# Down projection of a two-layer decoder: residual loads in half slices, kept weight blocks loaded with their partners, casts behind the sums, squares moved into slice 0's steps, and its norm in buffers of its own

## The chip, the cores and the metric

One core of one Trainium2 chip. TensorE (PE in the rows) multiplies; PEld is its weight load; VectorE (DVE), ScalarE (ACT) and GpSimd (POOL) do the elementwise work; SyncE (SP) and GpSimd issue the DMAs here. The metric is device microseconds of one execution, the median over runs. All times below are microseconds (us).

## The reference, cut to what matters

The program is one step of a two-layer decoder in fp32. Layer 0 is an mLSTM mixer, layer 1 an attention with forget gates; each is followed by the same kind of feed-forward block, and between the layers a shared key/value projection is made from the normed result of layer 0:

```
h = h + mixer_l(rmsnorm(h))                       # l = 0: mLSTM, l = 1: attention
h = h + swiglu(rmsnorm(h), w_gate_up[l], w_down[l])
        # gu = xn @ w_gu ;  (silu(gu[:, :2816]) * gu[:, 2816:]) @ w_d
after layer 0:  k, v, lf from  rmsnorm(h, norm_kv) @ w_kvf
after layer 1:  y = rmsnorm(h, norm_final)
```

The model width is 1024, the hidden width 2816. There are 1104 tokens: 64 of the sample group, 16 meta tokens, 1024 of the prompt.

## The kernel before, in words

**Tiling.** Activations lie transposed, width on the 128 partitions: the residual H of a token slice is a tile of 128 x 8 x 368 (8 chunks of the width, 368 tokens). There are three slices, t = 0, 1, 2. The program's names for the tiles of H are vA in layer 0 and Ht in layer 1 (in the issue order vA_83, vA_84, vA_85 are the areas of slices 0, 1, 2). An fp32 product is made of three fast ones: each operand is split into a high part (a cast on ACT, L331) and a low part (a subtraction on DVE, L332), and hi*hi, hi*lo, lo*hi are accumulated in PSUM.

**Down stage.** `ffn` runs twice. Its last part is the product with w_down, a list of 61 steps; each step is 24 matmuls (4 output chunks x 2 contraction chunks x 3 products, L1949). Steps 0 to 38 compute slices 1 and 2 by a scheme of Strassen's kind: seven "rounds" named r2, r5, r3, r1, r6, r7, r4 of five steps each, with four plain steps between (5, 6, 17, 18). A round multiplies sums of hidden slices (made earlier and put into DRAM as hA) with sums of weight blocks. Steps 39 to 60 are slice 0, plain, in two halves of the width. A step whose entry has an `out` ends an accumulation: DVE adds the four PSUM banks into H (L1492). A step with `lead` takes fresh banks, and there are four banks, so the lead step after an out step waits for these adds.

**What each step issues, in this order:** the split of the weight block needed two steps later (`w_split`: cast on ACT, low part on DVE); the split of the hidden block needed two steps later (`h_split`) and the load of the block three after it (`h_load`, POOL's queue, tile hr, three buffers with the tag ny, so that a load waits for the low part of the block three before it); the sum of the next weight block where the round needs one (`w_sum`, DVE, L1493), ahead of the matmuls in a step without `out`, behind the adds in a step with it; the 24 matmuls; the adds; the load of a weight block three ahead (`w_load`, SP's queue). The rounds r5, r1, r7, r4 need sums. The blocks that several rounds share are kept in the tile wx; five of them (`kept[1, q]`) are loaded in steps 3 to 7's calls of `w_load`, behind each call's own block.

**Residuals.** H was put into DRAM (hD) to make room, and comes back by POOL's queue at L1969: slice 1 is issued at step 1, slice 2 at step 3, slice 0 at step 8 of the program. PE, DVE and ACT run in the order in which the program is written; the order on the queues of POOL and SP is the scheduler's, which may put a DMA elsewhere.

**Squares and norm.** As the chunks of H are finished, a list `pend` collects their squares (`each`, which calls `add_sq`: ACT squares, L400 and L403, POOL adds into ns, L405, and DVE does the last add). One is taken from it at each step without an out before step 39 and two from there on. When a slice is complete its generator (`norm_x` in layer 0, `final` in layer 1) is appended, and `advance` takes one piece of it per step in steps 39 to 49, two from step 50. `norm_x` is a matmul with ones (L413), a square root, three reciprocals (L419), and for each chunk a multiplication, a cast and a subtraction (L425, L426, L428; for slice 0 four pieces of two chunks, L433, L439, L441, over the same three ny buffers). Behind the last step of layer 0 come the first products of the key/value projection (L269 to L271), whose weights are scaled by L325 and L326 and whose results are copied by L2054 and sent out by POOL.

Of the kernel before, what the change touches and what calls it, by code (L numbers as in the profile page):

```python
# [7 lines left out]
F32 = mybir.dt.float32  # L8
# [244 lines left out]
class Net:  # L253
# [153 lines left out]
    def norm_x(self, H, t, g, sp, pp, inplace=False, psum=False):  # L407
# [15 lines left out]
        for k in range(KT if psum else 0):  # L423
            y = pp.tile([P, 512], F32, name=self.uid("npy"), tag="n")[:, :n]
            nc.vector.tensor_tensor(out=y, in0=H[t][:, k], in1=r, op=ALU.mult)  # L425
            nc.scalar.copy(xh[:, k], y)  # L426
            yield
            nc.vector.tensor_tensor(out=xl[:, k], in0=y, in1=xh[:, k].bitcast(F32), op=ALU.subtract)  # L428
        for z in range(0 if psum else 4):
            ks = slice(2 * z, 2 * z + 2)  # L430
            y = H[t][:, ks] if inplace else self.ny(self.uid("ny"))[:, : 2 * n].rearrange("p (k n) -> p k n", k=2)
# [8 lines left out]
            yield  # L440
            nc.vector.tensor_tensor(out=xl[:, ks, :], in0=y, in1=xh[:, ks, :].bitcast(F32), op=ALU.subtract)  # L441
# [37 lines left out]
    def mlp(self, H, w, l, heads=None, cb=None, early=None):  # L479
# [8 lines left out]
        with self.pool(self.uid("nsp")) as sp, self.pool(self.uid("npp"), bufs=2, space=PSUM) as pn:  # L488
# [3 lines left out]
            def small(c, down=False):  # L492
                p = c.enter_context(self.pool(self.uid("small")))
                if down:
                    nq = p.tile([P, 1 if l else 2, SL], F32, name=self.uid("nq"))
                    self.nq = lambda x: self.nr if l and x else nq[:, x]
                    self.ny = lambda nm: p.tile([P, 2 * SL if l else max(2 * SL, 3 * 256)], F32, name=nm, tag="ny", bufs=3)
# [107 lines left out]
            with cw if not cb else ExitStack():  # L605
# [8 lines left out]
                if cb:  # L614
                    def after(t):
                        nc.gpsimd.dma_start(self.hD[:, :, TS[t][0] : TS[t][1]], H[t])
                        return self.norm_x(H, t, None, sp, pn, psum=t > 0)
# [847 lines left out]
def ffn(self, H, flat, l, weights, order, mix, small, each, after, end, early=None):  # L1465
# [10 lines left out]
    with self.pool(f"ffn{l}") as fp, self.pool(f"ffnp{l}", space=PSUM) as pp:  # L1476
# [220 lines left out]
        def w_load(i):  # L1697
            if i < len(ws):
# [18 lines left out]
                if 3 <= i < 3 + NR:  # L1717
                    keep_w(1, i - 3, 0, 0)
# [13 lines left out]

        def w_split(i):
            if i < len(ws):
                p = (i + max(0, min(3, (i - 19) // 5))) % 4
                wpart[i] = tuple(view(self.slots[y]) for y in (2 + p, LOW[p]))
                self.split(wraw.pop(i), *wpart[i])
# [143 lines left out]
        with fixed(E.DVE, E.Activation):  # L1881
# [24 lines left out]
            wr = dp.tile([P, KT * P], F32, name=f"wr{l}")  # L1906
            fin = None if after else self.final_setup(dp)
# [18 lines left out]
            for i, (wi, hi, lead, out) in enumerate(seq):  # L1926
# [9 lines left out]
                if todo and not out:  # L1936
                    w_sum(todo + 1)
# [25 lines left out]
                if todo and out:  # L1963
                    w_sum(todo + 1)
                if todo:
                    w_load(todo + 3)
                if i in (1, 3, 8):
                    y = {1: 1, 3: 2, 8: 0}[i]
                    nc.gpsimd.dma_start(H[y], self.hD[:, :, TS[y][0] : TS[y][1]])  # L1969
                for _ in range(0 if i < NX else 1 if i < NX + NC else 2):  # L1970
                    advance()
                if not out:
                    for _ in range(1 if i < NX else 2):
# [996 lines left out]
```

## Time and profile before

| | |
|---|---|
| three runs | 2869.14, 2859.06, 2856.49 us |
| median | 2859.06 us |
| profiled execution: time, span | 2863.41 us, 2861.7 us (1.7 us outside of the span) |
| granted clock of TensorE, mean | 0.989 |
| PE busy | 2755.9 us, 96% |
| DVE, ACT, POOL busy | 1869.1, 1317.8, 1105.6 us |
| DMA | 415.06 MB, mean 145 GB/s |
| down stage of layer 0, profile time | about 1003 to 1255 us, then the tail up to about 1300 |
| down stage of layer 1, profile time | about 2574 to 2849 us |

Rows of a timeline read: start, duration, engine, line, operation, output tile <- input tiles, shape, count, and in brackets the idle time of that engine just before and the instruction whose end ended it. Rows of windows give, for a stretch, the busy time of each engine with the number of instructions, the granted clock of TensorE (1.00 is full), the share of the DMA engines and the GB/s.

### The profile page before, as it was taken

To read this page: it belongs to the slowest core of one execution; us is meant where nothing else is said; L and a number is where in the kernel's file an instruction comes from. 1 tells how busy PE (TensorE), PEld (TensorE's weight loads), DVE (VectorE), ACT (ScalarE), POOL (GpSimd) and SP (SyncE) were. 2 spreads that over 40 slices of the span, in tenths; PEclk is the share of its full clock that TensorE was granted. 3 is DMA by queue.
4 is the path that set the end of the run, shared out by engine and by line. 5 is a ranking of instruction groups with operands and counts; after the bars stand their busy time and mean duration, and the time that the engine had idled before them with its cause. 6 is when DMAs were issued, how large, how long until landed. Compare 5 with 4: busy or idle time off the path is not lost. (4 is left out here: it accounts for less than half of the span.)

```text
span 2861.7 us, 54039 instructions
## 1 busy us (share of the span) xinstructions
PE 2755.9 (96%) x20390; PEld 2621.2 (92%) x20390; DVE 1869.1 (65%) x3790; ACT 1317.8 (46%) x2652; POOL 1105.6 (39%) x1612
## 2 busy tenths in 40 slices
PE   7999999999999989999999999999999999999998
PEld 7998988999999989999999888777999999998998
DVE  6044566688888766762465543777478888876673
ACT  6222464444444433442344454777344454443342
POOL 3042333065656312217573201455307566531220
PEclk9999999999999999999999999999999999999999
DMA  6157664122332385644453676452412223238463
GB/s 208 30 139 174 164 177 153 53 88 92 97 100 86 115 314 157 223 143 142 137 170 115 236 286 226 138 170 88 157 50 91 94 92 106 84 125 314 140 227 100
DMA packets 321207, 415.06 MB, mean 145 GB/s; under 512 B 30183, under 2 KB 244691, under 8 KB 319923
## 3 DMA queue, kind: packets, MB, share of 16 engines
q1 hardware_dynamic: 282114, 281.63, 30.9%
q0 software_dynamic: 38080, 129.43, 14.3%
q8 instruction: 160, 2.62, 0.4%
q14 instruction: 101, 0.82, 0.1%
q10 hardware_dynamic: 752, 0.57, 0.1%
HBM read 303.46 MB, written 108.07 MB: 144 GB/s over the span
## 5 line engine op out<-in xcount | busy, mean ns | idle before, releaser
L1949 PE MATMUL dps<-x0h,slot 128*128 128x368 f32 x1440 | 366.7, 334 | 19.0 <-DVE vA L1492 9.7
L1949 PEld LDWEIGHTS dps<-x0h,slot 128*128 128x128 f32 x1440 | 258.9, 190 | 22.4 <-issue 21.0
L332 DVE TENSOR_TENSOR slot<-slot,slot 128x256 fp32r<-128x256 f32 (+2 forms) x233 | 211.2, 908 | 68.3 <-ACT slot L331 63.5
L331 ACT CAST slot<-slot 128x256 fp32r<-128x256 f32 (+2 forms) x233 | 175.0, 754 | 163.7 <-PE m L1516 66.8
L1949 PE MATMUL dps<-x0l,slot 128*128 128x368 f32 x720 | 239.1, 332 | 1.0 <-DVE x0l L332 1.0
L1516 PE MATMUL m<-x1h,slot 128*128 128x368 f32 x640 | 180.0, 335 | 3.3 <-DVE ns L1493 0.9
L1516 PE MATMUL m<-x0h,slot 128*128 128x368 f32 x640 | 178.5, 329 | 0.0
L1949 PEld LDWEIGHTS dps<-x0l,slot 128*128 128x128 f32 x720 | 136.7, 190 | 1.3 <-DVE x0l L332 1.2
L111 POOL TENSOR_TENSOR slot<-Ht 128x256 f32<-128x256 f32 x80 | 75.4, 954 | 151.4 <-DMA Ht<-in_w_gate_up 79.8
L111 POOL TENSOR_TENSOR slot<-vA 128x256 f32<-128x256 f32 x80 | 75.4, 953 | 148.8 <-DMA vA<-in_w_gate_up 76.7
L1516 PE MATMUL m<-x2h,slot 128*128 128x368 f32 x480 | 132.3, 330 | 0.0
L1516 PEld LDWEIGHTS m<-x1h,slot 128*128 128x128 f32 x640 | 116.0, 188 | 12.4 <-DVE ns L1493 7.4
L332 DVE TENSOR_TENSOR slot<-Ht,slot 128x256 fp32r<-128x256 f32 (+3 forms) x101 | 91.5, 907 | 52.3 <-ACT slot L331 52.3
L332 DVE TENSOR_TENSOR slot<-vA,slot 128x256 fp32r<-128x256 f32 (+3 forms) x101 | 92.1, 913 | 50.3 <-ACT slot L331 50.3
L1669 POOL DMA_DIRECT2D hr<-hA x62 | 33.7, 543 | 217.6 <-DVE x0l L332 177.8
L1516 PEld LDWEIGHTS m<-x0h,slot 128*128 128x128 f32 x640 | 116.0, 188 | 0.0
L405 POOL TENSOR_TENSOR ns<-ns,nq 128x368 f32<-128x368 f32 x50 | 63.1, 1262 | 129.7 <-ACT nq L403 125.0
L1516 PE MATMUL m<-x1l,slot 128*128 128x368 f32 x320 | 105.5, 330 | 0.0
L1516 PE MATMUL m<-x0l,slot 128*128 128x368 f32 x320 | 105.4, 329 | 0.0
L2764 ACT ACTIVATE s<-s,nb 128x272 f32<-128x272 f32 (+7 forms) x126 | 98.8, 786 | 0.0
L2799 ACT COPY th<-tp 128x768 f32<-128x768 f32 (+1 forms) x80 | 73.5, 920 | 49.2 <-PE tp L2791 27.9
L1516 PE MATMUL m<-T_2h,slot 128*128 128x368 f32 x320 | 93.8, 334 | 0.0
(858 smaller groups left out, 9619.6 us busy)
## 6 DMA issues: line engine op xcount, KB each, us to landing
slot<-in_w_down SPq DMA_DIRECT2D x64, 512.0 KB, 4.4
hr<-hA POOLq DMA_DIRECT2D x62, 368.0 KB, 4.1
wraw<-in_w_in_a SPq DMA_DIRECT2D x40, 512.0 KB, 4.4
vA<-in_w_gate_up SPq DMA_DIRECT2D x40, 512.0 KB, 3.9
Ht<-in_w_gate_up SPq DMA_DIRECT2D x40, 512.0 KB, 4.0
wr<-in_w_down SPq DMA_DIRECT2D x32, 512.0 KB, 3.8
kp<-in_cache_k SPq DMA_DIRECT2D x32, 512.0 KB, 6.8
vp<-in_cache_v SPq DMA_DIRECT2D x32, 512.0 KB, 7.6
```

The costliest lines, as they stand in the source:

```text
L111: self.net.nc.gpsimd.tensor_tensor(out=o, in0=a, in1=b, op=op)
L331: self.nc.scalar.copy(hi, src)
L332: self.nc.vector.tensor_tensor(out=lo, in0=src, in1=hi.bitcast(F32), op=ALU.subtract)
L405: (nc.vector if x >= late else nc.gpsimd).tensor_tensor(out=s, in0=s, in1=sq, op=ALU.add)
L1516: nc.tensor.matmul(u.b[b][:, :SL], w[p][:, k], x[q][:, k], start=new and k == i == 0, stop=k == 1 and i == 2, skip_group_check=True)
L1669: nc.gpsimd.dma_start(hraw[j], src)
L1949: nc.tensor.matmul(o, w[:, k, ms], a[:, k], start=lead and k == x == 0, stop=k == 1 and x == 2, skip_group_check=True)
L2764: nc.scalar.activation(ss[z, u], ss[z, u], AF.Exp, bias=nb[:, z : z + 1], accum_out=sm[:, u, z : z + 1])
L2799: nc.scalar.copy(th.rearrange("p x z (u h q) -> p h (x z u) q", h=2, q=64)[:, :, :n], pt[:, :, :n])
```

## The change

1. The residual of slice 1 comes back in two halves of four chunks (program steps 1 and 11), that of slice 2 too (steps 2 and 7), that of slice 0 whole at step 24.
2. The five kept blocks are loaded by the calls of `w_load` that load the blocks of round r5 they are summed with, instead of by the calls 3 to 7.
3. `w_sum` always stands behind the matmuls and adds, and a new `w_high` issues the cast of the summed block right behind its sum, in the same step, unless the place in the ring of four shifts there.
4. No squares are taken before step 39; from there on two per step without an out.
5. The norm of slice 0 in layer 0 has two buffers of its own (wr and the pair nq) for its third and fourth piece, and each subtraction is issued one piece later.

```diff
-    def norm_x(self, H, t, g, sp, pp, inplace=False, psum=False):
+    def norm_x(self, H, t, g, sp, pp, inplace=False, psum=False, own=()):
...
+        behind = []
         for z in range(0 if psum else 4):
             ks = slice(2 * z, 2 * z + 2)
-            y = H[t][:, ks] if inplace else self.ny(self.uid("ny"))[:, : 2 * n].rearrange("p (k n) -> p k n", k=2)
+            y = own[z - 2] if z > 1 and own else self.ny(self.uid("ny"))
+            y = H[t][:, ks] if inplace else y[:, : 2 * n].rearrange("p (k n) -> p k n", k=2)
...
             nc.scalar.copy(xh[:, ks, :], y)
             yield
+            behind.append((ks, y))
+            for ks, y in behind[:1] if z else ():
+                nc.vector.tensor_tensor(out=xl[:, ks, :], in0=y, in1=xh[:, ks, :].bitcast(F32), op=ALU.subtract)
+            if z:
+                behind.pop(0)
+        for ks, y in behind:
             nc.vector.tensor_tensor(out=xl[:, ks, :], in0=y, in1=xh[:, ks, :].bitcast(F32), op=ALU.subtract)
...
+                    self.nqs = nq.rearrange("p k n -> p (k n)")
...
-                        return self.norm_x(H, t, None, sp, pn, psum=t > 0)
+                        return self.norm_x(H, t, None, sp, pn, psum=t > 0, own=() if t else self.spare)
...
-                if 3 <= i < 3 + NR:
-                    keep_w(1, i - 3, 0, 0)
+                if kind == "r" and r == 5:
+                    keep_w(1, q, 0, 0)
...
+        shift = lambda i: max(0, min(3, (i - 19) // 5))
+
+        def w_high(i):
+            if i < len(ws) and i not in wpart:
+                p = (i + shift(i)) % 4
+                wpart[i] = tuple(view(self.slots[y]) for y in (2 + p, LOW[p]))
+                nc.scalar.copy(wpart[i][0], wraw[i])
+
         def w_split(i):
             if i < len(ws):
-                p = (i + max(0, min(3, (i - 19) // 5))) % 4
-                wpart[i] = tuple(view(self.slots[y]) for y in (2 + p, LOW[p]))
-                self.split(wraw.pop(i), *wpart[i])
+                w_high(i)
+                sub(wpart[i][1], wraw.pop(i), wpart[i][0].bitcast(F32))
...
+            self.spare = wr, self.nqs
...
-                if todo and not out:
-                    w_sum(todo + 1)
...
-                if todo and out:
+                if todo:
                     w_sum(todo + 1)
-                if todo:
+                    if shift(todo) == shift(todo + 1):
+                        w_high(todo + 1)
                     w_load(todo + 3)
-                if i in (1, 3, 8):
-                    y = {1: 1, 3: 2, 8: 0}[i]
-                    nc.gpsimd.dma_start(H[y], self.hD[:, :, TS[y][0] : TS[y][1]])
+                for at, y, ks in ((1, 1, slice(0, 4)), (2, 2, slice(0, 4)), (7, 2, slice(4, 8)), (11, 1, slice(4, 8)),
+                                  (24, 0, slice(0, 8))):
+                    if at == i:
+                        nc.gpsimd.dma_start(H[y][:, ks], self.hD[:, ks, TS[y][0] : TS[y][1]])
...
                 if not out:
-                    for _ in range(1 if i < NX else 2):
+                    for _ in range(0 if i < NX else 2):
```

How the change moves instructions is seen in three places. The first is POOL's queue at the start of layer 0's down stage (vA_83, vA_84, vA_85 are the residual areas of slices 0, 1, 2; hr_4 to hr_10 are the hidden blocks of steps 4 to 10). Before:

```order
L1669 DMA hr_4_10103<-hA_2_5878 128x736
L1669 DMA hr_5_10114<-hT_1_5875 128x736
L1669 DMA hr_6_10150<-hT_2_5876 128x736
L1969 DMA vA_83<-hD 128x8x368
L1969 DMA vA_84<-hD 128x8x368
L1669 DMA hr_7_10184<-hA_5_5881 128x736
L1669 DMA hr_8_10216<-hA_5_5881 128x736
L1969 DMA vA_85<-hD 128x8x368
L1669 DMA hr_9_10247<-hA_5_5881 128x736
```

And now:

```order
L1986 DMA vA_84<-hD 128x4x368
L1678 DMA hr_4_10103<-hA_2_5878 128x736
L1678 DMA hr_5_10111<-hT_1_5875 128x736
L1678 DMA hr_6_10146<-hT_2_5876 128x736
L1986 DMA vA_83<-hD 128x8x368
L1986 DMA vA_84<-hD 128x4x368
L1678 DMA hr_7_10180<-hA_5_5881 128x736
L1986 DMA vA_85<-hD 128x4x368
L1678 DMA hr_8_10213<-hA_5_5881 128x736
L1678 DMA hr_9_10245<-hA_5_5881 128x736
L1986 DMA vA_85<-hD 128x4x368
```

Slice 0 (vA_83), which the program issues at step 24, still stands ahead of hr_7; the first half of slice 1 now stands ahead of hr_4; slice 2 is cut around hr_8 and hr_9. In layer 1 the queue has the same order.

The second place is ACT in layer 0, where the squares of slice 1 begin (ns and nq are the targets of the squares, slot the weights' high parts, x0h the hidden blocks'). Before, in round r7:

```order
L331 CAST x0h_5420<-hr_24_10808 128x736
L400 ACTIVATE ns_4920<-vA_84 128x368
L331 CAST slot_4933<-wx_10177 128x1024
L331 CAST x0h_5420<-hr_25_10838 128x736
L403 ACTIVATE nq_10101<-vA_84 128x368
L331 CAST slot_4931<-wx_10177 128x1024
```

Now, in slice 0's steps:

```order
L1748 CAST slot_4931<-wr_10102 128x1024
L400 ACTIVATE ns_4920<-vA_84 128x368
L403 ACTIVATE nq_10101<-vA_84 128x368
L331 CAST x0h_5420<-hr_40_11333 128x736
L1748 CAST slot_4929<-slot_4927 128x1024
L403 ACTIVATE nq_10101<-vA_84 128x368 x2
L331 CAST T_2h<-hr_41_11364 128x736
```

The squares have left the rounds (one per step) for slice 0 (two per step), and the cast of the next weight block stands ahead of them.

The third place is DVE at the end of layer 0's down stage, the norm of slice 0. Before:

```order
L433 TENSOR_TENSOR ny_12277<-vA_83,nr_4921 128x736
L441 TENSOR_TENSOR x0l_12214<-ny_12277,x0h_12213 128x2x368
L433 TENSOR_TENSOR ny_12312<-vA_83,nr_4921 128x736
L441 TENSOR_TENSOR x0l_12214<-ny_12312,x0h_12213 128x2x368
L2348 TENSOR_REDUCE q_12859<-qi 128x8
```

Now:

```order
L435 TENSOR_TENSOR wr_10102<-vA_83,nr_4921 128x736
L445 TENSOR_TENSOR x0l_12216<-ny_12248,x0h_12215 128x2x368
L435 TENSOR_TENSOR nq_10101<-vA_83,nr_4921 128x736
L445 TENSOR_TENSOR x0l_12216<-wr_10102,x0h_12215 128x2x368
L2365 TENSOR_REDUCE q_12859<-qi 128x8
L449 TENSOR_TENSOR x0l_12216<-nq_10101,x0h_12215 128x2x368
```

The last two pieces write into wr and nq instead of ny, each subtraction follows the next multiplication, and the last one stands behind a reduction (qi is a small table that POOL makes for the attention).

## The prediction

> **What bounds the kernel now.** I read the page's busy times first, then the windows of the three stretches that the change touches.
>
> ```profile
> PE 2755.9 (96%) x20390; PEld 2621.2 (92%) x20390; DVE 1869.1 (65%) x3790; ACT 1317.8 (46%) x2652; POOL 1105.6 (39%) x1612
> ...
> 1003.00:1255.00 252.00, 235.35 (x1371) 232.94 (x1370) 177.13 (x209) 101.53 (x134) 49.90 (x69) 0.98 0.64 213
> 1255.00:1300.00 45.00, 38.80 (x272) 37.62 (x271) 28.22 (x42) 19.86 (x39) 9.55 (x37) 1.00 0.58 193
> 2574.00:2849.00 275.00, 259.73 (x1540) 257.76 (x1539) 176.11 (x198) 102.16 (x128) 50.68 (x65) 0.98 0.60 199
> ```
>
> PE does the work and the change takes no matmul away. So all it can win is PE's idle time in these stretches and the clock lost behind it. I therefore listed PE's timeline there and kept each row with an idle of 0.6 us or more (below it there are only four of 0.24 to 0.40).
>
> ```profile
> 1036.59 0.65 PE L1949 MATMUL dps<-T_2h,slot 128*128 128x368 f32 x1 [6.94 <-DVE vA L1492]
> 1133.99 0.41 PE L1949 MATMUL dps<-x0h,slot 128*128 128x368 f32 x1 [1.83 <-DVE vA L1492]
> 1159.67 0.65 PE L1949 MATMUL dps<-x0h,slot 128*128 128x368 f32 x1 [5.27 <-DVE vA L1492]
> 1228.83 0.41 PE L1949 MATMUL dps<-x0h,slot 128*128 128x368 f32 x1 [2.10 <-DVE vA L1492]
> 1259.14 0.61 PE L1949 MATMUL dps<-x0h,slot 128*128 128x368 f32 x2 [0.65 <-DVE slot L332]
> 1280.41 0.89 PE L413 MATMUL nps<-ns,ones 128*128 128x368 f32 x2 [2.47 <-DVE ns L405]
> 1298.35 0.39 PE L269 MATMUL tmps<-slot,x0h 128*128 128x256 f32 x1 [3.07 <-ACT vf L2054]
> ...
> 2589.11 0.44 PE L1949 MATMUL dps<-x0l,slot 128*128 128x368 f32 x1 [0.95 <-DVE x0l L332]
> 2606.97 0.65 PE L1949 MATMUL dps<-T_2h,slot 128*128 128x368 f32 x1 [5.71 <-DVE Ht L1492]
> 2704.17 0.41 PE L1949 MATMUL dps<-x0h,slot 128*128 128x368 f32 x1 [1.86 <-DVE Ht L1492]
> 2730.59 0.65 PE L1949 MATMUL dps<-x0h,slot 128*128 128x368 f32 x1 [6.10 <-DVE Ht L1492]
> ```
>
> They add to 22.3 us in layer 0 and 14.6 in layer 1: the lead steps 6, 29, 34 of both layers, step 50, one late weight block, and two waits in the tail. From 1133.99 to where step 34 was due (1159.67 - 5.27) are five steps of 4.08 us. A long idle costs a second time:
>
> ```profile
> 2606.00:2610.00 4.00, 3.03 (x10) 3.06 (x11) 3.30 (x6) 0.59 (x1) 0.54 (x1) 0.50 1.03 377
> 1300.00:1303.00 3.00, 3.00 (x16) 3.00 (x15) 0.00 (x0) 0.11 (x1) 3.00 (x23) 0.50 0.00 0
> ```
>
> After the idles of 5.71 and 3.07 the granted clock is 0.50; the stretch 1255 to 1300, which holds the 2.47, shows 1.00. I price it at 1.7 us: some 3.4 us at half speed.
>
> **Part A, residuals and kept blocks (step 6).** The adds of step 5 stand behind the low part of hr_7 on DVE, and hr_7 lands late:
>
> ```profile
> 1010.61 0.92 DVE L332 TENSOR_TENSOR x0l<-vA,x0h 128x736 fp32r<-128x736 f32 x1
> 1035.07 0.92 DVE L332 TENSOR_TENSOR x0l<-hr,x0h 128x736 fp32r<-128x736 f32 x1 [7.91 <-ACT x0h L331]
> ...
> 1034.23 0.80 ACT L331 CAST x0h<-hr 128x736 fp32r<-128x736 f32 x1 [8.33 <-DMA hr<-hA]
> ...
> 1014.83 1.78 POOL L1969 DMA_DIRECT2D vA<-hD  x2 [7.50 <-ACT x0h L331]
> 1018.14 0.56 POOL L1669 DMA_DIRECT2D hr<-hA  x1 [1.52 <-DVE x0l L332]
> ...
> DMA packets 8925, 21.51 MB, mean 347 GB/s; under 512 B 704, under 2 KB 1904, under 8 KB 8920
> q0 software_dynamic: 2040, 9.00, 40.2%
> wx<-in_w_down SPq DMA_DIRECT2D x10, 512.0 KB, 17.6
> hr<-hA POOLq DMA_DIRECT2D x11, 368.0 KB, 6.0
> ```
>
> (The last four are the DMA view of 1000 to 1062.) Issued at 1018.14, hr_7 landed 16.1 us later, where the median of its kind is 6.0: ahead of it in POOL's queue stood two whole residuals of 1472 KB (128 x 8 x 368 words). The order of the changed queue shows that the same bytes still stand ahead of hr_7: slice 0 was not moved behind it, only half of slice 1 (736 KB) went ahead of hr_4. That half writes over the area that the low part of a weight block leaves just ahead of 1010.61, so neither it nor hr_4 to hr_6 behind it can issue before. POOL's queue moves 9.00 MB in 62 us, 145 GB/s; so half a residual and hr_4 (1104 KB, 1.13 MB) take 7.8 us: hr_4 lands near 1018.4, its low part is done 1.7 us later (0.80 + 0.92), at 1020.1. Step 4 is due at 1036.59 - 6.94 - 2 x 4.08 = 1021.5. It just holds. hr_7's buffer comes free with that low part, some 2 us later than before. Against this, the kept blocks' loads of steps 3 to 5 (3 x 512 KB, 4.5 us at 347 GB/s) move behind hr_7. Bounds per layer: 4.5 earlier or 3 later. I take 0.5 later in each, since what stands ahead of it in its own queue is unchanged: **-1.0**. In layer 1 the 0.95 at 2589.11 (a weight block loading beside hr_4 to hr_6, which now start later) goes: **+0.95**, or nothing.
>
> **Part B, squares out of the rounds (steps 29, 34).** From r7 on a step with a sum is a ping-pong of DVE and ACT.
>
> ```profile
> 1123.05 2.00 DVE L1493 TENSOR_TENSOR slot<-wx,slot 128x1024 f32<-128x1024 f32 x1
> 1166.51 1.22 DVE L1493 TENSOR_TENSOR slot<-slot,wx 128x1024 f32<-128x1024 f32 x1
> 1170.91 1.22 DVE L1493 TENSOR_TENSOR slot<-slot,wx 128x1024 f32<-128x1024 f32 x1
> ...
> 1122.31 1.66 POOL L405 TENSOR_TENSOR ns<-ns,nq 128x368 f32<-128x368 f32 x1 [1.87 <-ACT nq L403]
> ...
> 2693.24 2.00 DVE L1493 TENSOR_TENSOR slot<-wx,slot 128x1024 f32<-128x1024 f32 x1
> ```
>
> Without squares it repeats every 4.40 us (1166.51 to 1170.91), 0.32 more than PE's 4.08; with a POOL add on top the sum takes 2.00 instead of 1.22. Four sums of layer 0 are so stretched (two ahead of step 29), five in layer 1. Without them the adds that release step 34 come 4 x 0.78 = 3.1 earlier, of which 1.6 already at step 29, and 5 x 0.78 = 3.9. I take **+3.0 and +3.75**. The 4.40 stays, so step 34 still waits some 3.8 us, longer than the 3.07 that lost the clock; I leave that loss in place (3.4 for both layers if it goes). The cast behind its sum buys nothing in the rounds: the order on ACT and DVE is there the same.
>
> **Part C, slice 0's steps.** With a norm piece ahead of the weight's cast, the steps took 4.45 us:
>
> ```profile
> 1205.61 1.23 DVE L332 TENSOR_TENSOR slot<-slot,slot 128x1024 fp32r<-128x1024 f32 x1 [1.49 <-ACT slot L331]
> 1210.06 1.22 DVE L332 TENSOR_TENSOR slot<-slot,slot 128x1024 fp32r<-128x1024 f32 x1 [1.48 <-ACT slot L331]
> ```
>
> That eats the two steps' lead and ends in the 2.10 of step 50 and the 0.65. Now the cast comes ahead of the piece, the 1.48 of waiting falls away, and both go: **+2.75**. What comes in are two squares a step in steps 39 to 47. The nearest rows are where two adds fell on two subtractions:
>
> ```profile
> 1175.38 1.93 DVE L332 TENSOR_TENSOR slot<-wr,slot 128x1024 fp32r<-128x1024 f32 x1
> 1177.23 1.70 DVE L332 TENSOR_TENSOR x0l<-hr,x0h 128x736 fp32r<-128x736 f32 x1
> ...
> 1174.49 1.74 POOL L405 TENSOR_TENSOR ns<-ns,nq 128x368 f32<-128x368 f32 x1 [2.10 <-ACT nq L403]
> 1176.73 1.42 POOL L405 TENSOR_TENSOR ns<-ns,nq 128x368 f32<-128x368 f32 x1
> ```
>
> The pair takes 3.5 us (1175.38 to 1178.9) instead of 2.0, under 4.08; I cost it at nothing, hidden under the matmuls. If the adds' whole times came on top (1.74 + 1.42 + 2.0 = 5.2), each of nine steps would be 1.1 late. The Trainium skill, "SBUF — State Buffer", section "SBUF: two separate sides", says that DVE with two SBUF inputs and GpSimd hold their shared ports as an exclusive lock, the loser fully blocked. That speaks against this move, and the trace agrees in kind (2.00 for 1.22). By it in full the sum is that of rival 3; by the pair's own row nothing is lost.
>
> **Part D, the tail of layer 0.** The third and fourth norm piece no longer wait for a ny buffer:
>
> ```profile
> 1296.27 0.93 DVE L433 TENSOR_TENSOR ny<-vA,nr 128x736 f32<-128x736 f32 x1 [3.83 <-DMA vD<-vf]
> ...
> 1298.32 2.89 POOL L2344 TENSOR_SCALAR_AFFINE_SELECT qi<-qi 128x8 f32<-128x8 f32 x16
> 1301.09 2.43 POOL L2346 TENSOR_SCALAR_AFFINE_SELECT qi<-qi 128x8 f32<-128x8 f32 x16
> ```
>
> The 3.07 at 1298.35 goes with its 1.7 of clock, but the last subtraction now stands behind a reduction that waits for these selects (over 5.3 us on POOL), which leaves 0.6 to 1.0 as I place them. I take **+4.0**, between nothing (the selects end as late as before) and 4.7. The 2.47 at 1280.41 waits for an add queued behind weight scalings; the work ahead of it is unchanged, but less crowded: **+1.3**, the middle of 0 and 2.5.
>
> **The sum.** -1.0 + 0.95 + 6.75 + 2.75 + 5.3 = 14.75 us of gain. The profiled execution took 2863.41 (span 2861.7 and 1.7 around it) and would take 2848.7; the median of the runs shown is 4.35 below it, 2859.06, which gives **2844**. 0.5%, about what can be told from no change, is 14.3 us: the forecast sits on that line.
>
> **The rivals.**
> 1. *The loads do relieve hr_7.* If its landing moves up by the 4.5 us of the kept blocks, step 6 idles 2.4 and 1.2, below 3.07, and the clock loss goes too: 2 x (4.5 + 1.7 + 0.5) = 13 more, 2831. For it: transfers of both queues share full engines here (share 1.03 in the window at 2606). Against it: hr_7's own queue still holds the residuals. The Trainium skill, "DMA: Bandwidth & Descriptors", "Issuing engines are not separate DMA queues", is for it, as transfers interleave on the same engines whoever issues them; no run here separates the two.
> 2. *The POOL queue turns against it: slower.* Place: the half residual ahead of hr_4. It decides once hr_4 lands after 1021.5 - 1.7 = 1019.8. If hr_4 then takes as long as hr_7 did (16.1), it lands at 1026.7, and hr_7, whose buffer it frees at 1028.4 instead of 1018.1, follows 10.3 us later than before; with half of that in layer 1 and a clock loss at step 4 in both, 10.3 + 5.2 + 3.4 = 18.9 us are lost beside the 15.75 gained: 2862.
> 3. *Squares and subtractions collide in slice 0.* 9 x 1.1 = 10 per layer, less one step of lead (4.1): 6 each, 2856.
> 4. *The tail stays as long*, because the reduction holds the last subtraction until the old time: 4 less, 2848. The order on DVE speaks for it; that only a part of the products needs that piece speaks against it.
>
> **Chances.** Forecast 0.42 (its own range 2838 to 2851), rival 1 0.23, rival 4 0.13, rival 3 0.12, rival 2 0.10. Faster by over 0.5% (below 2844.8): a little over half of the forecast and all of rival 1, 0.47. Slower by over 0.5% needs rivals 2 and 3 together or worse: 0.07. Within: 0.46. The range reaches from below rival 1 to just short of rival 2: 2827 to 2860.
>
> **What would show it.** Right: sums of 1.2 instead of 2.0 in r7 and r4, idles of about 0.3 at step 29 and 3.8 at step 34, none at step 50, still some 7 and 6 at step 6, under 1 where 3.07 stood. Wrong: an idle at step 4, at steps 41 to 52, or a wait for x0l in the tail; step 6 below 3 would mean rival 1.

## The result, and the profile after

The changed kernel takes 2843.06 us (median of five runs, 2837.88 to 2845.07) against 2858.81 of the kernel before beside it: 15.75 us less by the medians. The measured ratio is 0.9935 with a 95% interval of 0.9913 to 0.9957; the medians alone give 0.9945, and the means of the same runs are 18.6 apart. The forecast was 2844. The ratios in this document leave out one execution of undo_cast (3454.94) and one of squares_only (5168.71), two of the kernels below, whose granted clocks were 0.72 and 0.93.

The same three stretches in the windows of the changed kernel (start:end, length, busy time of PE, PEld, DVE, ACT and POOL with their counts, granted clock, DMA share, GB/s):

```profile
1003.00:1248.00 245.00, 234.84 (x1366) 231.55 (x1365) 174.29 (x208) 105.01 (x136) 49.88 (x69) 0.99 0.66 223
1248.00:1295.00 47.00, 46.78 (x350) 46.34 (x349) 28.94 (x49) 22.11 (x48) 21.88 (x99) 1.00 0.49 164
2560.00:2825.00 265.00, 254.29 (x1506) 251.26 (x1504) 171.03 (x192) 102.44 (x129) 46.89 (x63) 0.98 0.60 199
```

PE is as busy as before; the tail of layer 0 now has no hole (46.78 of 47.00). PE's timeline, each idle of 0.35 us or more in the two down stages and the tail:

```profile
1032.56 0.65 PE L1964 MATMUL dps<-T_2h,slot 128*128 128x368 f32 x1 [3.17 <-DVE vA L1501]
1038.74 0.41 PE L1964 MATMUL dps<-x0h,slot 128*128 128x368 f32 x1 [0.62 <-DVE vA L1501]
1055.58 0.43 PE L1964 MATMUL dps<-x0h,slot 128*128 128x368 f32 x1 [0.51 <-ACT x0h L331]
1056.97 0.44 PE L1964 MATMUL dps<-x0l,slot 128*128 128x368 f32 x1 [0.96 <-DVE x0l L332]
1061.45 0.41 PE L1964 MATMUL dps<-x0h,slot 128*128 128x368 f32 x1 [0.35 <-DVE vA L1501]
1155.01 0.64 PE L1964 MATMUL dps<-x0h,slot 128*128 128x368 f32 x1 [3.75 <-DVE vA L1501]
...
2564.62 0.44 PE L1964 MATMUL dps<-x0l,slot 128*128 128x368 f32 x1 [1.09 <-DVE x0l L332]
2569.75 0.44 PE L1964 MATMUL dps<-x0l,slot 128*128 128x368 f32 x1 [0.82 <-DVE x0l L332]
2584.82 0.46 PE L1964 MATMUL dps<-T_2h,slot 128*128 128x368 f32 x1 [2.93 <-DVE Ht L1501]
2591.00 0.41 PE L1964 MATMUL dps<-x0h,slot 128*128 128x368 f32 x1 [0.39 <-DVE Ht L1501]
2608.17 0.44 PE L1964 MATMUL dps<-x0l,slot 128*128 128x368 f32 x1 [0.72 <-DVE x0l L332]
2612.65 0.40 PE L1964 MATMUL dps<-x0h,slot 128*128 128x368 f32 x1 [0.36 <-ACT x0h L331]
2706.08 0.65 PE L1964 MATMUL dps<-x0h,slot 128*128 128x368 f32 x1 [3.79 <-DVE Ht L1501]
```

Beside the rows of before: step 34 idles 3.75 and 3.79 where 5.27 and 6.10 stood (3.8 was foretold), step 29 and step 50 are gone, the 2.47 and 3.07 of the tail are gone. At step 6 stand 3.17 and 2.93 instead of 6.94 and 5.71, which was not foretold, and there are new waits of 0.4 to 1.1 around it. The larger ones, 0.5 to 1.1, come mostly from weight blocks that land late: their rows name a cast or a low part of a hidden block (x0h, x0l), but on ACT and DVE those stand behind the work on a weight block, which waits for its load. DVE's and ACT's timelines of the same kernel:

```profile
1052.44 1.22 DVE L1502 TENSOR_TENSOR wx<-slot,wx 128x1024 f32<-128x1024 f32 x1 [3.73 <-DMA slot<-in_w_down]
...
2566.55 1.05 ACT L1748 CAST slot<-wr 128x1024 fp32r<-128x1024 f32 x1 [15.43 <-DMA wr<-in_w_down]
```

**A measure for single stages.** Medians of whole runs scatter by several us, and single executions differ by some us in code that no edit touches. I therefore measure each kernel's two stages in its profiled execution: "stage 0" from the first down matmul of layer 0 to the first matmul of the attention's projections behind the tail, "stage 1" from the first to the last down matmul of layer 1. Before: 354.7 (1005.32 to 1359.98) and 272.7 (2575.63 to 2848.32). After: 340.2 and 268.4, that is 14.5 and 4.3 less, 18.8 together. The two profiled spans differ by 25.5; the other 6.7 lie in unchanged code (1.1 ahead of stage 0, 4.9 between the stages, 0.7 behind) and are no gain of the change; the medians say 15.75. A stage itself can differ by some 2 us without any cause in the edit: behind the same short idles the clock of TensorE drops in one kernel and stays in another (last section), and one drop costs about 1.8 (step 6 of the kernel before, with the clock at half, takes 5.9 instead of 4.08: from 1036.59 to 1042.77, less 0.25 of waiting). Differences of stages of that size are not read here.

### The profile page after: what moved, and what is told of

It is laid out like the page before. It is cut to its first block, busy times and chain, and to the rows that moved or that the text cites. A ratio compares the mean times of both kernels' runs of the same rounds, so it can differ in the third digit from the quotient of the medians.

```text
span 2836.2 us, 54037 instructions
## 1 busy us (share of the span) xinstructions
PE 2750.0 (97%) x20390; PEld 2615.8 (92%) x20390; DVE 1864.8 (66%) x3790; ACT 1319.0 (47%) x2652; POOL 1104.0 (39%) x1616
## 5 line engine op out<-in xcount | busy, mean ns | idle before, releaser
L332 DVE TENSOR_TENSOR slot<-slot,slot 128x512 fp32r<-128x512 f32 (+3 forms) x175 | 139.4, 798 | 21.1 <-ACT slot L331 16.1
L331 ACT CAST slot<-slot 128x512 fp32r<-128x512 f32 (+3 forms) x175 | 114.3, 656 | 78.9 <-PE m L1525 67.1
L332 DVE TENSOR_TENSOR slot<-Ht,slot 128x256 fp32r<-128x256 f32 (+2 forms) x100 | 90.9, 910 | 50.8 <-ACT slot L331 50.8
L332 DVE TENSOR_TENSOR slot<-vA,slot 128x256 fp32r<-128x256 f32 (+2 forms) x100 | 90.6, 907 | 51.2 <-ACT slot L331 51.2
L1748 ACT CAST slot<-slot 128x1024 fp32r<-128x1024 f32 x58 | 60.8, 1049 | 90.1 <-PE dps L1964 44.5
L2816 ACT COPY th<-tp 128x768 f32<-128x768 f32 (+1 forms) x80 | 73.5, 920 | 46.1 <-PE tp L2808 25.5
```

The lines of the kernel that those rows point to most:

```text
L331: self.nc.scalar.copy(hi, src)
L332: self.nc.vector.tensor_tensor(out=lo, in0=src, in1=hi.bitcast(F32), op=ALU.subtract)
L1748: nc.scalar.copy(wpart[i][0], wraw[i])
L2816: nc.scalar.copy(th.rearrange("p x z (u h q) -> p h (x z u) q", h=2, q=64)[:, :, :n], pt[:, :, :n])
```

## The experiments

Twelve further kernels ran, each timed beside the kernel before. Ratios are to the kernel before; idles are PE's at the step named, layer 0 / layer 1.

| kernel | median us | ratio (95%) | stage 0 | stage 1 | step 6 | step 29 | step 34 |
|---|---|---|---|---|---|---|---|
| before | 2858.81 | | 354.7 | 272.7 | 6.94 / 5.71 | 1.83 / 1.86 | 5.27 / 6.10 |
| changed | 2843.06 | 0.9935 (0.9913 to 0.9957) | 340.2 | 268.4 | 3.17 / 2.93 | 0.21 / 0.25 | 3.75 / 3.79 |
| undo_halves | 2843.52 | 0.9939 (0.9917 to 0.9961) | 342.0 | 268.6 | 4.17 / 4.51 | under 0.3 | 3.75 / 3.79 |
| undo_kept | 2842.37 | 0.9930 (0.9905 to 0.9955) | 339.7 | 268.5 | 3.26 / 1.66 | under 0.3 | 3.74 / 3.78 |
| undo_loads | 2844.68 | 0.9929 (0.9904 to 0.9954) | 341.0 | 268.6 | 6.93 / 6.61 | under 0.3 | 3.70 / 3.79 |
| undo_squares | 2854.57 | 0.9976 (0.9964 to 0.9987) | 346.3 | 273.8 | 2.18 / 2.90 | 2.60 / 2.64 | 5.43 / 5.67 |
| undo_cast | 2856.88 | 0.9983 (0.9970 to 0.9997) | 352.4 | 269.3 | 2.03 / 0.57 | under 0.3 | 3.70 / 3.78 |
| undo_norm | 2847.17 | 0.9955 (0.9938 to 0.9973) | 344.3 | 268.5 | 3.02 / 2.56 | under 0.3 | 3.70 / 3.79 |
| cast_only | 2858.62 | 0.9987 (0.9976 to 0.9999) | 350.2 | 275.2 | 5.67 / 6.39 | 2.60 / 2.64 | 6.96 / 7.31 |
| squares_only | 2858.09 | 0.9982 (0.9970 to 0.9994) | 355.2 | 268.2 | 5.69 / 6.44 | under 0.3 | 3.70 / 3.79 |
| pool_order | 2831.80 | 0.9893 (0.9873 to 0.9912) | 333.8 | 262.7 | under 0.3 | under 0.3 | 3.70 / 3.79 |
| h_first | 2830.84 | 0.9881 (0.9858 to 0.9903) | 334.4 | 262.1 | 3.71 / 1.22 | under 0.3 | under 0.3 |
| both | 2816.84 | 0.9851 (0.9829 to 0.9872) | 330.3 | 256.2 | under 0.3 | under 0.3 | under 0.3 |
| both_kept | 2819.53 | 0.9849 (0.9830 to 0.9869) | 330.7 | 256.1 | 2.00 / 2.06 | under 0.3 | under 0.3 |

### The loads: halves, kept blocks, and both undone

From the changed kernel, the residuals issued whole again:

```diff
-                for at, y, ks in ((1, 1, slice(0, 4)), (2, 2, slice(0, 4)), (7, 2, slice(4, 8)), (11, 1, slice(4, 8)),
-                                  (24, 0, slice(0, 8))):
+                for at, y, ks in ((1, 1, slice(0, 8)), (3, 2, slice(0, 8)), (8, 0, slice(0, 8))):
```

> The changed kernel with the residuals issued whole again (at steps 1, 3 and 8), the kept blocks still loaded with their partners. Theory 1 (the half of slice 1 that no weight block lies under goes out before the DMA engines are full, and so 736 KB less stand ahead of hr_7): the idle at step 6 goes back from 3.17 to near the 6.94 of before in layer 0 and from 2.93 to near 5.71 in layer 1, layer 0's stage (first down matmul to the first matmul of the attention's projections, 340.2 in the changed kernel) becomes 3 to 4 longer, layer 1's (first to last down matmul, 268.4) 2.5 to 3. Theory 2 (the kept blocks' loads that moved behind made the room): both idles stay near 3, both stages within 1.

From the changed kernel, the kept blocks at their old place:

```diff
-                if kind == "r" and r == 5:
-                    keep_w(1, q, 0, 0)
+                if 3 <= i < 3 + NR:
+                    keep_w(1, i - 3, 0, 0)
```

> The changed kernel with the kept blocks loaded by the calls 3 to 7 again, the residuals still in halves. Theory 1 (the half residual did it): step 6 still idles 3 to 4 in both layers, and the new waits of 0.5 to 1.1 for late weight blocks at 1055.58, 1056.97, 2564.62 and 2569.75 get smaller or go: both stages within 1 of 340.2 and 268.4, or shorter. Theory 2 (the kept blocks made the room): step 6 goes back to 6 to 7, layer 0 becomes 3 to 4 longer, layer 1 2.5 to 3.

Each alone left the stages within 1.8 us, and the 1.8 (the halves undone, layer 0) holds a drop of the clock behind idles of 0.52 and 0.96 that the changed kernel, with 0.51 and 0.96 at the same steps, does not show. Neither theory had it: undoing the halves put 1.0 and 1.6 back at step 6, not 3.8 and 2.8; undoing the kept blocks put almost nothing back there in layer 0 (3.26 for 3.17). So both were undone together:

> The changed kernel with both edits of the loads undone: residuals whole, kept blocks by the calls 3 to 7. Undoing the halves alone put 1.0 and 1.6 back at step 6, undoing the kept blocks alone nothing in layer 0 (3.26) and 0.7 in layer 1 (1.66 + 1.94 over two steps). If either of the two edits alone makes most of the room: with both undone step 6 goes back to 6 to 7 in layer 0 and 5 to 6 in layer 1, the stages 3 to 5 longer than 340.2 and 268.4. If neither does (the room comes from the casts standing behind the sums): step 6 stays at 4 to 4.5, the stages within 2.

Step 6 did go back to 6.93 and 6.61, and yet the stages are only 0.8 and 0.2 longer. PE's timeline of that kernel, all its idles of 0.35 or more in the two stages:

```profile
1042.59 0.65 PE L1964 MATMUL dps<-T_2h,slot 128*128 128x368 f32 x1 [6.93 <-DVE vA L1501]
1162.50 0.42 PE L1964 MATMUL dps<-x0h,slot 128*128 128x368 f32 x1 [3.70 <-DVE vA L1501]
2579.12 0.44 PE L1964 MATMUL dps<-x0l,slot 128*128 128x368 f32 x1 [0.79 <-DVE x0l L332]
2597.92 0.65 PE L1964 MATMUL dps<-T_2h,slot 128*128 128x368 f32 x1 [6.61 <-DVE Ht L1501]
2717.85 0.41 PE L1964 MATMUL dps<-x0h,slot 128*128 128x368 f32 x1 [3.79 <-DVE Ht L1501]
```

The small waits around step 6 are not there. Up to step 13 this kernel idles 6.93 and 7.40; the changed one 3.17 + 0.62 + 0.51 + 0.96 + 0.35 = 5.6 and 1.09 + 0.82 + 2.93 + 0.39 + 0.72 + 0.36 = 6.3. The two edits of the loads cut one long wait into several short ones: from 1007 to 1051 the DMA engines are full in both kernels (a share of 1.01 at 365 GB/s with the loads undone, 1.03 at 386 in the changed kernel), and until about step 12 all the same bytes must pass. Together the two edits are worth about 1 us of the 18.8, no more than stages differ by themselves.

Why hr_7 came earlier at all, in POOL's, DVE's and ACT's timelines of the changed kernel:

```profile
1000.69 0.76 POOL L1986 DMA_DIRECT2D vA<-hD  x1 [6.41 <-DMA hA<-vA]
1002.12 0.54 POOL L1678 DMA_DIRECT2D hr<-hA  x1 [0.68 <-issue]
...
1015.06 1.66 POOL L1986 DMA_DIRECT2D vA<-hD  x2 [8.90 <-ACT slot L1748]
1019.41 0.55 POOL L1678 DMA_DIRECT2D hr<-hA  x1 [2.70 <-DVE x0l L332]
...
1010.59 1.22 DVE L1502 TENSOR_TENSOR slot<-vA,slot 128x1024 fp32r<-128x1024 f32 x1
...
1029.97 0.81 ACT L331 CAST x0h<-hr 128x736 fp32r<-128x736 f32 x1 [0.93 <-DMA hr<-hA]
```

The half residual ahead of hr_4 went out at 1000.69, ten us ahead of the low part (1010.59) that reads the weight block in the area of slice 1. So it cannot be the half that lies under that block (the block fills the first 1024 words of the area): it is the second one, issued in the program at step 11, and the scheduler put it first. No weight block held it; its row waits for an older transfer out of the area (hA<-vA). It starts while the engines still have room (a share of 0.78 from 1000 to 1004, 1.00 from 1004 to 1008), and hr_7 lands 10.6 us after its issue (1019.41 to 1029.97) instead of 16.1. Counted from each kernel's first down matmul, it is issued 2.4 later than before and lands 3.2 earlier.

### POOL's queue in program order

The changed kernel, with the order of POOL's instructions fixed in the down stage as those of PE, DVE and ACT are:

```diff
-        with fixed(E.DVE, E.Activation):
+        with fixed(E.DVE, E.Activation, E.Pool):
```

> The changed kernel with POOL's queue in the order in which the program is written, too: slice 0's residual (1472 KB) then goes out at step 24, and ahead of hr_7 stand 736 KB alone. If what stands ahead of hr_7 in its queue makes it late: it lands some 4 earlier, step 6 idles under 0.5 in both layers, without half clock; stages 4 to 5 shorter than 340.2 and 268.4. If the engines' common bandwidth makes it late, or its buffer: step 6 still idles 2 to 3. A loss elsewhere: POOL's adds of the squares now stand in line with its loads, idles of 0.5 or more in steps 40 to 50.

Slice 0's residual then really goes out at step 24. The stages fall by 6.4 and 5.7, more than expected; 2831.80, ratio 0.9893. The idle at step 6 is under 0.3; of the stretch there remain one late block in layer 1 and step 7, which waits for the adds of step 6:

```profile
1030.50 0.41 PE L1964 MATMUL dps<-x0h,slot 128*128 128x368 f32 x1 [1.75 <-DVE vA L1501]
...
2564.33 0.44 PE L1964 MATMUL dps<-x0l,slot 128*128 128x368 f32 x1 [0.90 <-DVE x0l L332]
2582.51 0.41 PE L1964 MATMUL dps<-x0h,slot 128*128 128x368 f32 x1 [1.94 <-DVE Ht L1501]
```

This is the difference between moving a wait and moving bytes: 1472 KB leave the full stretch (at the 383 GB/s that the engines moved from 1007 to 1051 in the kernel before, 3.9 us), and the half clock behind step 6 goes with them (the granted clock is 1.00 from 1030 to 1034). How much of it is the bytes and how much the order is not separated: in this run the second halves of slices 2 and 1 go out later, too, 36.6 and 49.3 after the first down matmul (1036.99, 1049.65), where the last two halves of the changed kernel's queue went 15.7 and 26.7 after it (1019.96, 1030.88). What the diff says of slice 0 (step 24) and what the queue did in the changed kernel (ahead of hr_7) were two things.

### The squares

From the changed kernel, one square per step in the rounds again:

```diff
-                    for _ in range(0 if i < NX else 2):
+                    for _ in range(1 if i < NX else 2):
```

> The changed kernel with one square per step taken in the rounds again. If the squares' adds on POOL stretched the sums: sums of 2.0 in r7 and r4 again, step 29 idles 1.6 more, step 34 some 1.5 more in layer 0 and 2.2 more in layer 1, the stages 3.1 and 3.5 to 3.9 longer than 340.2 and 268.4. If the gain there came from the casts or from the earlier hr_7: the stages within 1 of the changed kernel's.

The stages became 6.1 and 5.4 longer, against 3.1 and 3.5 to 3.9 expected. The idles at steps 29 and 34 account for 2.4 + 1.7 and 2.4 + 1.9 of it. The rest was not traced in full; a part of it is the clock, which dropped here behind the idles of 2.60 and 2.64 at step 29 (last section). That these idles are larger than before the change, 1.83 and 1.86, has a cause that the cast done alone shows, below.

### The cast behind the sum

From the changed kernel, the early cast taken out (the sums stay where they are):

```diff
-                    if shift(todo) == shift(todo + 1):
-                        w_high(todo + 1)
```

> The changed kernel without the cast behind the sum; each block is cast in the step that splits it, as before. If the cast ahead of the norm's pieces is what freed step 50: the norm pieces of slice 0's steps put 4.45 us per step back, idles of 2 to 2.8 in steps 50 to 58 of layer 0, stage 340.2 + 2.7. If the norm's later start already freed them: nothing there. If the cast also made the room at step 6: an idle of 6 to 7 there in both layers, otherwise 3 to 3.5. In the rounds nothing: step 34 idles 3.75 and 3.79 as now.

Layer 0's stage became 12.2 longer, layer 1's 0.9: far more than the 2.7 that the first theory gave, and at another place. ACT's and DVE's timelines of that kernel in slice 0's steps, and PE's idles behind it:

```profile
1229.97 0.47 ACT L426 CAST x1h<-npy 128x368 fp32r<-128x368 f32 x1 [1.06 <-DVE npy L425]
1230.33 0.51 ACT L400 ACTIVATE ns<-vA 128x368 f32<-128x368 f32 x1
1230.74 0.50 ACT L403 ACTIVATE nq<-vA 128x368 f32<-128x368 f32 x1
1231.14 1.04 ACT L1748 CAST slot<-slot 128x1024 fp32r<-128x1024 f32 x1
...
1226.27 1.23 DVE L1502 TENSOR_TENSOR slot<-slot,slot 128x1024 fp32r<-128x1024 f32 x1 [1.48 <-ACT slot L1748]
...
1232.21 1.23 DVE L1502 TENSOR_TENSOR slot<-slot,slot 128x1024 fp32r<-128x1024 f32 x1 [2.28 <-ACT slot L1748]
...
1238.15 1.87 DVE L1502 TENSOR_TENSOR slot<-wr,slot 128x1024 fp32r<-128x1024 f32 x1 [2.27 <-ACT slot L1748]
...
1240.52 1.59 PE L413 MATMUL nps<-ns,ones 128*128 128x368 f32 x2 [5.56 <-DVE x1l L428]
1281.62 1.57 PE L413 MATMUL nps<-ns,ones 128*128 128x368 f32 x2 [3.54 <-DVE ns L405]
```

With the norm's pieces and the squares ahead of each weight's cast, a step repeats every 5.94 us (1226.27 to 1232.21 to 1238.15), against PE's 4.08; the waits for the cast are 2.28 instead of the 1.48 of before. ACT's rows show the queue: a norm piece, two squares of slice 2, and only then the weight's cast. The squares and the norm of slice 1 fall into the same steps by the change's move. The clock behind 5.56 and 3.54 is at half, too (0.50 and 0.59 in windows of 4 us). In the rounds the cast did nothing, as foretold: step 34 is at 3.70 and 3.78.

### Cast alone and squares alone

The same two edits made on the kernel before, each without the rest of the change:

> The kernel before with the casts behind the sums alone: residuals whole, kept blocks by the calls 3 to 7, squares in the rounds, norm over three ny buffers with each subtraction right behind its piece. If the cast ahead of the norm's pieces pays by itself: the idles of 2.10 and 0.65 at step 50 and behind it go, layer 0's stage (354.7 before) is 2.5 to 3 shorter, layer 1's (272.7) the same. If it pays only as a cover for the squares in slice 0: both stages within 1 of the kernel before.

> The kernel before with the squares moved into slice 0's steps alone, the casts where they were. If the move pays by itself: 3.0 and 3.8 shorter stages than 354.7 and 272.7. If it needs the early cast as its cover (without it the changed kernel's layer 0 became 12.2 longer, with idles of 5.56 and 3.54 at the norm's matmuls): layer 0's stage 4 to 9 longer than 354.7, with idles of 3 or more before the ones-matmuls of L413, layer 1's 3 to 4 shorter.

Both came out within 0.2% of the kernel before. Cast alone wins 4.4 in layer 0 (the 2.10, the 0.65 and the 2.47 are gone, and the 3.07 is 2.34 with a granted clock of 1.00 behind it, while steps 29 and 34 lose 2.5) and loses 2.6 in layer 1: step 34 idles 6.96 and 7.31 instead of 5.27 and 6.10. The reason stands in the DVE and POOL timelines of that kernel:

```profile
1124.10 1.70 DVE L332 TENSOR_TENSOR x0l<-hr,x0h 128x736 fp32r<-128x736 f32 x1
1125.73 1.21 DVE L1501 TENSOR_TENSOR slot<-wx,slot 128x1024 f32<-128x1024 f32 x1
...
1160.43 0.54 DVE L405 TENSOR_TENSOR ns<-ns,nq 128x368 f32<-128x368 f32 x1 [1.65 <-ACT nq L403]
...
1123.42 1.60 POOL L405 TENSOR_TENSOR ns<-ns,nq 128x368 f32<-128x368 f32 x1 [1.66 <-ACT nq L403]
```

POOL's add now meets the low part of the hidden block (1.70 instead of 0.92) and no longer the sum (1.21): about the same 0.78 each time, but at every square, six of them ahead of step 34 (with starts 1124.10, 1129.20, 1134.37, 1145.68, 1150.85, 1155.95) where the kernel before had four. Two more are 1.6 us; about another 0.9 is the last add, on DVE, which now waits 1.65 for its square. Together 2.4, of which 0.8 shows at step 29 and 1.7 at step 34.

Squares alone win 4.5 in layer 1 and lose 0.6 in layer 0, where idles of 5.55 and 3.54 stand ahead of the norm's matmuls, the same as without the cast above. So the two edits cover each other: the cast ahead of the squares keeps slice 0's steps under PE's, and the squares' leaving keeps the cast from stretching the rounds.

### The norm's buffers

From the changed kernel, the last pieces over the ny buffers again and each subtraction right behind its piece (`own` empty, `behind` emptied at once).

> The changed kernel with the norm of slice 0 over the three ny buffers again and each subtraction right behind its piece. If the buffers were what held the tail: the fourth piece waits for the copy's DMA again, an idle of 3.07 and some 1.7 of half clock behind it come back, layer 0's stage is 4 to 5 longer than 340.2, layer 1's the same. If the tail became short because the work ahead of it ended earlier: the stage stays within 1.5.

Stage 0 is 4.1 longer, stage 1 the same, and the wait is back, in PE's and DVE's timelines:

```profile
1289.92 0.39 PE L269 MATMUL tmps<-slot,x0h 128*128 128x256 f32 x1 [2.87 <-ACT vf L2070]
...
1287.83 0.93 DVE L435 TENSOR_TENSOR ny<-vA,nr 128x736 f32<-128x736 f32 x1 [3.31 <-DMA vD<-vf]
```

Only 2.9 of the 4.1 lie in the tail, behind the last down matmul (80.8 instead of 77.9), which is the idle of 2.87 alone: the half clock that was expected behind it did not come (1.00 from 1290 to 1294). The other 1.2 lie in the down steps, which this edit leaves alone; the clock dropped there behind idles of 0.59 and 0.95 (0.68 from 1058 to 1062).

### Two further edits

What is left in the changed kernel, apart from step 6, is step 34, and the prediction gave its cause: sum, cast, low part of the weight, low part of the hidden block, 4.40 us a step. In this run the hidden block's split goes ahead of the weight's, so that its low part fills DVE's wait for the cast, and the early cast is kept for the plain blocks alone:

```diff
-                while wj < wneed[k]:
-                    wj += 1
-                    w_split(wj)
-                    todo = wj
                 while hj < hneed[k]:
                     hj += 1
                     h_split(hj)
                     h_load(hj + 3)
+                while wj < wneed[k]:
+                    wj += 1
+                    w_split(wj)
+                    todo = wj
...
-                    if shift(todo) == shift(todo + 1):
+                    if shift(todo) == shift(todo + 1) and ws[min(todo + 1, len(ws) - 1)][0] == "p":
```

> The changed kernel with the split of the hidden block ahead of the split of the weight block in each step, and the early cast kept for the plain blocks alone. The low part of the hidden block then falls into DVE's wait for the cast of the summed block. If the chain sum, cast, low part, low part (4.40) is what holds step 34: the repeat falls to about 1.22 + 1.15 + 1.2 = 3.6, under PE's 4.08, the idles of 3.75 and 3.79 and the half clock behind them go, and each stage is 5 to 5.5 shorter than 340.2 and 268.4. If the four banks' eight adds or late loads hold it: the idles stay over 2, the stages within 2.

The idles at step 34 are gone, the stages 5.8 and 6.3 shorter. DVE's timeline of that kernel in round r7:

```profile
1149.12 1.22 DVE L1502 TENSOR_TENSOR slot<-slot,wx 128x1024 f32<-128x1024 f32 x1
1150.25 0.92 DVE L332 TENSOR_TENSOR x0l<-hr,x0h 128x736 fp32r<-128x736 f32 x1
1151.45 1.22 DVE L1502 TENSOR_TENSOR slot<-slot,slot 128x1024 fp32r<-128x1024 f32 x1 [0.28 <-ACT slot L1748]
1152.59 1.22 DVE L1502 TENSOR_TENSOR slot<-slot,wx 128x1024 f32<-128x1024 f32 x1
```

From sum to sum 3.47 us (1149.12 to 1152.59), under PE's 4.08; the wait for the cast is 0.28 where it was 1.2.

Both edits together:

> The changed kernel with the hidden block's split first and with POOL's queue in program order, together. If step 34's chain and step 6's late load are independent: each stage is shorter by the sum of the two single runs, 340.2 - 5.7 - 6.4 = 328 and 268.4 - 6.3 - 5.7 = 256, some 2821 to 2824 in time, ratio to the kernel before 0.982 to 0.987. If the room gained at step 6 is lost again at the next waits (the late weight blocks of round r5): stages of 331 or more and 259 or more.

2816.84, ratio 0.9851; stages 330.3 and 256.2 (328 and 256 by the sum of the two). It beats both kernels, by 44.6 us the one before beside it (2861.45) and by 26 the median of the changed one, which was measured at another time beside 2858.81. Last, the kept blocks at their old place in that kernel:

> The run with both further edits, and the kept blocks loaded by the calls 3 to 7 again. If the waits left in round r5 (0.47 + 0.65 + 0.54 in layer 0, 0.91 + 0.80 + 0.66 + 0.51 in layer 1) come from the kept blocks' loads standing among the late weight blocks: they go, stages 1.5 shorter than 330.3 and 2.5 shorter than 256.2. If these loads then crowd the hidden blocks again: step 6 idles 1 or more, the stages as long as or longer than those.

The waits in round r5 went, step 6 idles 2.00 and 2.06 again, and the stages are the same (330.7 and 256.1): once more the same bytes, waited for at another place.

## Why the prediction was right

**Total and sign.** 2844 was forecast and 2843.06 measured, with the chances almost even between faster and no change; 0.65% by the ratio, 0.55% by the medians, is over the 0.5% line by a little, and the upper end of the interval (0.9957) is not. The sum of the terms was 14.75; the two stages of the profiled executions gave 18.8, the medians 15.75. The idles that the prediction staked itself on came out: about 0.2 at step 29, 3.8 at step 34, none at step 50, under 1 where 3.07 stood. That the forecast lies within 1 us of the median is luck: the five runs spread over 7 us, and the terms fall 4 short of the stages. Of the 18.8, 7.2 lie in layer 0's down steps (the terms gave 5.25), 7.2 in its tail (5.3) and 4.3 in layer 1 (4.2).

**Part A** was put at -1.0 + 0.95, and it is worth about +1 (undo_loads: 0.8 and 0.2), less than a stage differs by itself. The size, next to nothing, was right, the way there was not. Two steps failed. "That half writes over the area that the low part of a weight block leaves just ahead of 1010.61, so neither it nor hr_4 to hr_6 behind it can issue before": it was the other half, which no weight block held, and it went out at 1000.69. The order shows tile and size of a transfer, not which half; I took the one that the program issues first. And "0.5 later in each": hr_7's buffer did come free some 2 us later (2.4), but it landed 3.2 earlier. That this gained nothing is because the idle time came back as late weight blocks; the 0.95 at 2589.11 did not go, it is 1.09. The prediction priced one transfer's place in one queue and left out that the stretch as a whole is full (383 GB/s from 1007 to 1051), where the next transfer is late instead.

**Part B** said 3.0 and 3.75. The idles at steps 29 and 34 together fell by 3.14 and 3.92, and step 34 kept the 3.75 and 3.79 that were foretold, with the clock at about half behind it (0.59 and 0.50 in windows of 4 us). Step 29, which the prediction counts among the lead steps, takes no fresh banks; it goes on in those that the adds of step 28 read, and waits for them all the same. Taken back from the changed kernel, the edit is worth more (6.1 and 5.4), since there the early cast makes POOL's adds meet the low part of a hidden block at every square (1.70 instead of 0.92), six times ahead of step 34.

**Part C** said 2.75, and both idles are gone. But "the cast behind its sum buys nothing in the rounds" is true only without squares there (cast_only: 1.7 and 1.2 lost at step 34), and "I cost it at nothing, hidden under the matmuls", of the squares in slice 0, holds only beside the cast: without it stage 0 is 12.2 longer. The terms were added as if they were independent; taken alone, cast and squares give nothing to speak of (0.9987 and 0.9982).

**Part D** said 4.0 and 1.3, and the tail, from the last down matmul to the end of stage 0, went from 85.1 to 77.9, 7.2 less. The 2.47 fell to 0.22, 2.25 instead of 1.3, and the rest, the 3.07 with the half clock behind it, is 5.0 instead of 4.0. The 2.25 is booked at the wrong edit: that idle stands at 0.22 with the cast alone and at 3.54 in the two kernels that move the squares without it (undo_cast, squares_only), so the cast brings it, and not the norm. The own buffers are worth 2.9 when the clock does not drop (undo_norm), and 5.0 with the drop of the kernel before. The last subtraction behind the selects cost nothing. POOL's and DVE's timelines of the changed kernel:

```profile
1282.46 2.43 POOL L2363 TENSOR_SCALAR_AFFINE_SELECT qi<-qi 128x8 f32<-128x8 f32 x16
...
1284.92 0.40 DVE L2365 TENSOR_REDUCE q<-qi 128x8 f32<-128x128 f32 x1 [4.98 <-POOL qi L2363]
1285.24 1.16 DVE L449 TENSOR_TENSOR x0l<-nq,x0h 128x736 fp32r<-128x736 f32 x1
```

It does wait 4.98 us for them, as its place in the order said, and no matmul waited for it: PE has no idle of 0.35 or more there. The 0.6 to 1.0 left in the sum for it were too much.

**The rivals.** Rival 1 (hr_7 relieved) was half right: it landed earlier, step 6 fell to 3.17 and 2.93, but the clock still dropped (0.58 in the window of 4 us behind the first), and the gain was eaten by the next waits; pool_order, with slice 0 out of the stretch, gains 6.4 and 5.7. Rival 2 did not happen, since hr_4 was not held (issued at 1002.12). Rival 3, the collision in slice 0: POOL's adds do meet subtractions there (low parts of hidden blocks of 1.34 to 1.44 instead of 0.92, from 1180 to 1211), but with the cast in place no idle of 0.35 or more follows. Without the cast layer 0 loses 12.2; subtractions of up to 2.38 stand there from 1180 to 1210, and behind them the 5.94 us a step of the queue on ACT. How the 12.2 divide between the two is not shown. Rival 4 did not happen.

## What to carry to other kernels

Where the DMA engines were full over a stretch (383 GB/s for 44 us), moving loads within it moved the wait (stages 0.8 and 0.2 apart, though step 6 went from 3.17 to 6.93), and the run that took a whole residual out of it gained 6.4 and 5.7 us; so look where the queue puts a load, not where the program issues it. A chain between two engines (sum, cast, subtraction) is shortened by putting an independent instruction into the wait in its middle: here 0.92 us of other work, put into a wait of 1.2, made a step 0.9 us shorter and won 5.8 and 6.3 us. Edits that are each other's cover are to be tested alone and together, since neither has a price of its own. And a stage that came out 1 or 2 us longer is not yet an effect of the edit: look first whether the clock dropped behind an idle that both kernels have.

## What the runs showed of the hardware

Which idle costs clock is not told by its length. An idle of 2.60 (undo_squares, step 29 of layer 0) showed a granted clock of 0.71 in the window of 4 us behind it, and one of 2.64 (layer 1) 0.57; the kernel with the cast alone idles the same 2.60 and 2.64 at the same steps and showed 1.00 behind both (from 1136 and from 2700). An idle of 2.03 (undo_cast, step 6) showed 0.57, one of 2.87 (undo_norm, the tail) 1.00. Even the pair 0.52 and 0.96 (undo_halves) showed 0.67 where the pair 0.51 and 0.96 of the changed kernel showed 1.00. The windows, in this order: undo_squares twice, cast_only, undo_cast, undo_halves, the changed kernel:

```profile
1138.00:1142.00 4.00, 3.82 (x17) 3.85 (x18) 2.83 (x6) 1.40 (x2) 1.30 (x2) 0.71 0.77 260
2696.00:2700.00 4.00, 3.35 (x12) 3.38 (x13) 2.98 (x6) 0.93 (x1) 0.55 (x1) 0.57 0.63 205
1136.00:1140.00 4.00, 3.36 (x20) 3.39 (x21) 2.98 (x6) 0.94 (x1) 1.43 (x2) 1.00 0.76 238
1032.00:1036.00 4.00, 3.73 (x13) 3.76 (x14) 2.81 (x6) 1.28 (x2) 1.27 (x2) 0.57 1.04 387
1056.00:1060.00 4.00, 3.04 (x11) 2.87 (x11) 4.00 (x5) 3.94 (x5) 1.08 (x2) 0.67 0.49 157
1056.00:1060.00 4.00, 3.04 (x19) 3.03 (x19) 4.00 (x6) 3.79 (x5) 1.07 (x2) 1.00 0.51 155
```

The Trainium skill, "TensorE: Matmul & The Clock Gate", section "What's actually happening", gives an idle window of about 3.4 us that runs free of the kernel. That the same idle loses clock in one kernel and not in another agrees with a free-running window; that idles of 2.0 to 2.6 lose clock is shorter than its figure, and here the rows decide. What decides in a single case no run here shows.
